# Four of eight gate and up quads as seven block products, and half of the other quads' low parts made by an adding DMA

## The chip, the cores and the metric

The kernel runs on one core of a Trainium2 chip. The metric is the device time of one execution in microseconds (us), as the median of several runs; a profile is taken of one more execution.

## What is computed

A trunk of two layers over 256 tokens with a model width of 2048, in float32. Layer 0 has a gated mixer and a pooling mixer, layer 1 latent attention; the change touches neither. Each layer ends in a SwiGLU, and that is where the change is made:

```python
D_MODEL = 2048; SEQ = 256
D_FF = -(-8 * D_MODEL // (3 * 256)) * 256      # 5632

def swiglu(h, w_gate, w_up, w_down):
    return (jax.nn.silu(h @ w_gate) * (h @ w_up)) @ w_down

for layer in range(DEPTH):                     # DEPTH = 2
    ...
    x = x + mix
    x = x + swiglu(rmsnorm(x, g_ffn[layer]), w_gate[layer], w_up[layer], w_down[layer])
return rmsnorm(x, g_final)
```

## The kernel before, in words

**Split operands.** TensorE multiplies in the type `F32R`. To keep float32 accuracy every operand is a pair: a high part `wh`, the value rounded to `F32R`, and a low part `wl`, the value minus its high part. ScalarE (ACT) writes the high part and VectorE (DVE) the low part (`split_raw`, lines 95 to 104, in pieces of up to 1024 columns). A product of two pairs is three matmuls: high by high, high by low, low by high (`token_product`, lines 205 to 209; every one of them 128 by 128 by 512 columns here).

**Quads.** Gate and up are computed in *columns*: a column is 512 of the 5632 outputs of gate and the same 512 of up, for all 256 tokens. There are 11 columns in each layer, cut into parts of 4, 4 and 3 (`PARTS`); after each part the rows of `w_down` that belong to it are multiplied (`into_trunk`). The 2048 inputs of a column are taken in eight *quads* j = 0 to 7 of 256 inputs. A quad is a 2 by 2 matrix of input blocks (x11, x21, x12, x22, 128 tokens by 128 inputs each) times a 2 by 2 matrix of weight blocks (b11, b12, b21, b22, 128 inputs by 512 outputs each). Done directly it takes eight block products, 24 matmuls. The quads in `SEVEN` (3, 5, 7) are done by Winograd's form with seven block products, 21 matmuls: `quad_seven` (lines 471 to 485) makes the sums t1, t3, t2, t4 of weight blocks on DVE and splits them too, and `put_pair` (lines 253 to 270) makes the sums s1 to s4 of input blocks once per layer, in the tile `forms` (it has the name `ckv` in the profile). Four accumulators c11, c12, c21, c22 hold the column (tiles `mm`) and four more, p1, p6, p5, p7 (tiles `sm`), the shared products; eight additions on DVE (`L520`) put them together at the column's end, with copies out of PSUM on ACT before them (`L519`).

**What sets the order.** One generator, `chunks_of`, walks over all quads of gate and up and all chunks of `w_down` in the order of use. For each it issues one load of 1024 KB into `raw` (three buffers) from the SP queue and splits it, and it runs two chunks ahead of the matmuls. High and low parts have six buffers each. A buffer is handed out in the order in which buffers come free, so each piece takes the place of the sixth piece before it, as soon as the matmuls that read that one are through.

```python
    whs = pool("whs", 6)
    wls = pool("wls", 6)
    ...
            while len(ready) <= AHEAD and todo:
                src, split = todo.pop(0)
                raw = raws.tile([P, 2 * SPLIT], F32, name="raw")
                nc.sync.dma_start(out=raw, in_=src)
                ready.append(split(raw))
```

After a column its hidden block is turned by transposes on TensorE into two `sm` tiles of PSUM and split from there into `hid` (`L581`, `L582`). These wait in a list, `pending`, and are emitted in the next column: after quads 1 and 2 two each, if so many are there (line 554). The order on each engine is set by a scheduler when the program is built; it is fixed in the program.

Of the kernel before, what the change touches and what calls it, by code (L numbers as in the profile page):

```python
# [21 lines left out]

SEVEN = (3, 5, 7)
AHEAD = 2
# [8 lines left out]
def trunk(ctx: ExitStack, tc: tile.TileContext, a: dict, out: bass.AP):  # L33
# [210 lines left out]
    def into_trunk(w, k0, nk, moving, g, sums, chunks=None, scaled=None):  # L244


        def turn(m, src):

            def put(pt):
                for j in range(2):  # L250
                    split_into(xs[:, m + j, :], pt[:, j * T:(j + 1) * T], gain(g, m + j))

            def put_pair(pt):
                xg = ev([2, T])
                for j in range(2):
                    nc.scalar.activation(out=xg[:, j, :], in_=pt[:, j * T:(j + 1) * T], func=AF.Copy, scale=gain(g, m + j))
                nc.scalar.activation(out=xs[:, m:m + 2, :T], in_=xg, func=AF.Copy)
                nc.vector.tensor_tensor(out=xs[:, m:m + 2, T:], in0=xg, in1=xs[:, m:m + 2, :T].bitcast(F32), op=ALU.subtract)
                if m // 2 not in SEVEN:
                    return  # L260
                a11, a21, a12, a22 = xg[:, 0, :P], xg[:, 0, P:], xg[:, 1, :P], xg[:, 1, P:]
                f = ev([4, P])
                s1, s2, s3, s4 = (f[:, i, :] for i in range(4))
                nc.vector.tensor_tensor(out=s1, in0=a21, in1=a22, op=ALU.add)
                nc.vector.tensor_tensor(out=s2, in0=s1, in1=a11, op=ALU.subtract)
                nc.vector.tensor_tensor(out=s3, in0=a11, in1=a21, op=ALU.subtract)
                nc.vector.tensor_tensor(out=s4, in0=a12, in1=s2, op=ALU.subtract)
                q = scaled["forms"][:, SEVEN.index(m // 2), :, :, :]
                nc.scalar.activation(out=q[:, 0, :, :], in_=f, func=AF.Copy)
                nc.vector.tensor_tensor(out=q[:, 1, :, :], in0=f, in1=q[:, 0, :, :].bitcast(F32), op=ALU.subtract)  # L270

            turned(src, put_pair if scaled else put)
# [52 lines left out]
    def forms():  # L325

        return big.tile([P, len(SEVEN), 2, 4, P], F32R, name="ckv")

# [141 lines left out]

    def quad_seven(raw):

# [13 lines left out]

    def quad_eight(raw):
        parts = split_raw(raw, 2048)
        return dict(zip(("b11", "b12", "b22", "b21"), (block(parts, i) for i in range(4))))

    def chunks_of(layer):
# [4 lines left out]
        for n in PARTS:  # L496
# [3 lines left out]
            for c in range(4):  # L500
                for i in range(0, 4 * n, 4):
                    todo.append((wd[c, :, (4 * at + i) * 512:(4 * at + i + 4) * 512], lambda raw: split_raw(raw, 2048)))
            at += n
        ready = []
        for n in range(len(todo)):
            while len(ready) <= AHEAD and todo:
                src, split = todo.pop(0)
                raw = raws.tile([P, 2 * SPLIT], F32, name="raw")
                nc.sync.dma_start(out=raw, in_=src)
                ready.append(split(raw))  # L510
            yield ready.pop(0)

    def feed_forward(layer, sums, scaled, g_next):
# [7 lines left out]
        for part, n in enumerate(PARTS):  # L521
            hid = hidden()
            for c in range(n):
# [8 lines left out]
                for j in range(KD // 2):  # L532
# [4 lines left out]
                    if j not in SEVEN:  # L537
                        for xk, bg, bu in (((x11, x21), "b11", "b12"), ((x12, x22), "b21", "b22")):
                            for x_t, pg, pu in ((xk[0], c11, c12), (xk[1], c21, c22)):
                                sum_into(pg, x_t, w[bg], False)  # L540
                                sum_into(pu, x_t, w[bu], pu is c22 and xk[0] is x12 and j == max(set(range(KD // 2)) - set(SEVEN)))
                    else:
                        if j == SEVEN[0]:
                            p1, p6, p5, p7 = (ps_sm.tile([P, 512], F32, name="sm") for _ in range(4))
                        q = forms[:, SEVEN.index(j)]
                        s1, s2, s3, s4 = ((q[:, 0, i, :], q[:, 1, i, :]) for i in range(4))
                        sum_into(c11, x12, w["b21"], lasting)
# [4 lines left out]
                        sum_into(p5, s1, w["t1"], lasting)  # L552
                        sum_into(p7, s3, w["t3"], lasting)
                    if j in (1, 2):
                        next_pending(2)
                    if j == KD // 2 - 2:
                        e22 = copy(c22)
# [266 lines left out]
```

## Time and profile before

| | |
|---|---|
| median of 3 runs | 1942.32 us (1941.19 to 1942.67) |
| profiled execution, its own time | 1942.75 us |
| its span in the profile | 1940.9 us, so 1.85 us lie around the span |
| TensorE (PE) busy | 1921.9 us, 99% of the span, 9110 matmuls |
| DVE, ACT, POOL busy | 75%, 55%, 1% |
| loads on the SP queue | 53.5% of the 16 DMA engines' span |

The duration of a matmul in the profile covers its whole way through the array, so several overlap; what one costs is the distance between two starts. The same holds for DVE and ACT: an instruction starts a little before the one ahead of it is down as ended. A row of a timeline gives the start, the duration, the engine, the line, the operation, tiles out and in, and in square brackets the idle time before it and what ended it. "High" and "low" rows of weights are `L101` and `L102`.

### The profile page before, as it was taken

What the parts mean: (1) busy time and instruction counts of PE and PEld (TensorE: products, weight loads), DVE (VectorE), ACT (ScalarE), POOL (GpSimd) and SP (SyncE); (2) the same over time, 40 slices, a digit from 0 to 9 for tenths busy, and PEclk for the clock granted to TensorE, in tenths of its full rate; (3) what the DMA queues carried; (4) which work ended last, traced back from release to release, by engine and by line L of the source; (5) the groups of instructions that cost most, each with busy time, mean ns of one, the idle gap of its engine ahead of it and who ended that gap; (6) DMA issues with size and microseconds to landing.
All of it is one profiled execution on the core that took longest, in us unless ns stands there. A gap on an engine that the chain in (4) does not pass through costs nothing.

```text
span 1940.9 us, 23494 instructions
## 1 busy us (share of the span) xinstructions
PE 1921.9 (99%) x9110; PEld 1610.7 (83%) x9110; DVE 1448.9 (75%) x1793; ACT 1066.0 (55%) x1424; POOL 10.1 (1%) x26
## 2 busy tenths in 40 slices
PE   9999999999999999999999999999999999999997
PEld 7888888888888888888889988888888888888886
DVE  6685589985688965887676755899856889658884
ACT  6554666563456643555554755665634566435562
POOL 0000000000000000000000000000000000000000
PEclk9999999999999999999999999999999999999998
DMA  8565545565555555456455235455655556655562
GB/s 310 174 215 197 195 160 209 195 213 194 179 195 195 210 201 190 179 195 217 175 194 175 96 135 184 171 208 188 214 194 183 187 199 211 210 181 177 208 242 87
DMA packets 54688, 370.94 MB, mean 191 GB/s; under 512 B 6320, under 2 KB 7856, under 8 KB 10544
## 3 DMA queue, kind: packets, MB, share of 16 engines
q1 hardware_dynamic: 52560, 364.93, 53.5%
q10 hardware_dynamic: 2016, 4.51, 0.6%
q8 instruction: 71, 1.16, 0.2%
q14 instruction: 41, 0.34, 0.0%
HBM read 367.32 MB, written 2.10 MB: 190 GB/s over the span
## 4 chain that ended last, share of the span: by engine, by line
PE 97%; DVE 1%; DMA 1%; ACT 1%; issue 0%; POOL 0%; ACTq 0%; SPq 0%; POOLq 0%
PE mm L207 24%; PE mm L209 24%; PE mm L208 24%; PE mm L131 5%; PE sm L209 3%; PE sm L208 3%; PE sm L207 3%; PE mm L132 2%; PE sm L241 2%; PE mm L363 1%; PE mm L364 1%; PE mm L137 1%; PE mm L362 1%; PE mm L136 1%; PE mm L138 1%; DMA raw<-in_w_v 1%
## 5 line engine op out<-in xcount | busy, mean ns | idle before, releaser
L102 DVE TENSOR_TENSOR wl<-raw,wh 128x1024 fp32r<-128x1024 f32 (+1 forms) x692 | 802.7, 1165 | 342.6 <-ACT wh L101 338.9
L101 ACT ACTIVATE wh<-raw 128x1024 fp32r<-128x1024 f32 (+1 forms) x692 | 695.1, 1013 | 538.4 <-PE mm L209 458.8
L207 PE MATMUL mm<-wh,xs 128*128 128x512 f32 x1012 | 395.2, 391 | 0.0
L209 PE MATMUL mm<-wh,xs 128*128 128x512 f32 x1012 | 393.9, 389 | 0.0
L208 PE MATMUL mm<-wl,xs 128*128 128x512 f32 x1012 | 393.8, 389 | 0.0
L207 PE MATMUL mm<-wh,hid 128*128 128x512 f32 x960 | 375.5, 391 | 0.0
L209 PE MATMUL mm<-wh,hid 128*128 128x512 f32 x960 | 373.6, 390 | 0.0
L208 PE MATMUL mm<-wl,hid 128*128 128x512 f32 x960 | 373.6, 389 | 0.0
L209 PEld LDWEIGHTS mm<-wh,xs 128*128 128x128 f32 x1012 | 189.9, 188 | 39.5
L207 PEld LDWEIGHTS mm<-wh,xs 128*128 128x128 f32 x1012 | 190.0, 188 | 39.0
L208 PEld LDWEIGHTS mm<-wl,xs 128*128 128x128 f32 x1012 | 190.0, 188 | 38.8
L209 PEld LDWEIGHTS mm<-wh,hid 128*128 128x128 f32 x960 | 180.2, 188 | 37.5
L207 PEld LDWEIGHTS mm<-wh,hid 128*128 128x128 f32 x960 | 180.2, 188 | 37.0 <-ACT hid L581 0.3
L208 PEld LDWEIGHTS mm<-wl,hid 128*128 128x128 f32 x960 | 180.3, 188 | 36.7
L102 DVE TENSOR_TENSOR wl<-sums,wh 128x1024 fp32r<-128x1024 f32 x132 | 161.3, 1222 | 63.6 <-ACT wh L101 63.6
L101 ACT ACTIVATE wh<-sums 128x1024 fp32r<-128x1024 f32 x132 | 139.4, 1056 | 126.1 <-DVE sums L475 96.6
L131 PE MATMUL mm<-xs,wh 128*128 128x512 f32 x375 | 133.8, 399 | 0.0
L132 PE MATMUL mm<-xs,wl 128*128 128x256 f32 x375 | 104.8, 280 | 0.0
L131 PEld LDWEIGHTS mm<-xs,wh 128*128 128x128 f32 x375 | 70.4, 188 | 15.9 <-DVE xs L170 0.3
L475 DVE TENSOR_TENSOR sums<-raw 128x1024 f32<-128x1024 f32 x66 | 80.5, 1220 | 1.0 <-DMA raw<-in_w_gu 0.5
L520 DVE TENSOR_TENSOR ev<-sm,ev 128x512 f32<-128x512 f32 x110 | 75.6, 688 | 2.6
L207 PE MATMUL sm<-wh,ckv 128*128 128x512 f32 x198 | 77.0, 389 | 0.0
(198 smaller groups left out, 1920.2 us busy)
## 6 DMA issues: line engine op xcount, KB each, us to landing
raw<-in_w_gu SPq DMA_DIRECT2D x176, 1024.0 KB, 4.8
raw<-in_w_d SPq DMA_DIRECT2D x88, 1024.0 KB, 4.8
raw<-in_w_o SPq DMA_DIRECT2D x32, 1024.0 KB, 4.8
raw<-in_w_v SPq DMA_DIRECT2D x11, 1024.0 KB, 6.6
raw<-in_w_z SPq DMA_DIRECT2D x8, 1024.0 KB, 5.0
raw<-in_w_u SPq DMA_DIRECT2D x8, 1024.0 KB, 4.8
raw<-in_w_q SPq DMA_DIRECT2D x6, 1024.0 KB, 4.9
raw<-in_w_ckv SPq DMA_DIRECT2D x4, 1024.0 KB, 4.8
```

Source lines behind the costliest of these rows:

```text
L101: nc.scalar.activation(out=wh[:, :m], in_=raw[:, o:o + m], func=AF.Copy)
L102: nc.vector.tensor_tensor(out=wl[:, :m], in0=raw[:, o:o + m], in1=wh[:, :m].bitcast(F32), op=ALU.subtract)
L131: nc.tensor.matmul(ps, lhsT=wh, rhs=mv, start=first, stop=False)
L132: nc.tensor.matmul(ps[:, :T], lhsT=wl, rhs=mv[:, :T], start=False, stop=last)
L136: nc.tensor.matmul(ps[:, :T], lhsT=wh, rhs=mv[:, :T], start=first, stop=False)
L137: nc.tensor.matmul(ps[:, :T], lhsT=wh, rhs=mv[:, T:], start=False, stop=False)
L207: nc.tensor.matmul(ps, lhsT=hi, rhs=wh, start=first, stop=False)
L208: nc.tensor.matmul(ps, lhsT=hi, rhs=wl, start=False, stop=False)
L209: nc.tensor.matmul(ps, lhsT=lo, rhs=wh, start=False, stop=last)
L241: nc.tensor.transpose(pt[:, o:o + P], src(t, j), ident)
L475: sub = lambda out, p, q: nc.vector.tensor_tensor(out=out, in0=p, in1=q, op=ALU.subtract)
L520: add = lambda out, p, q: nc.vector.tensor_tensor(out=out, in0=p, in1=q, op=ALU.add)
```

## The change

Four things are changed.

1. `SEVEN` becomes (2, 4, 6, 7), so that four quads of a column take seven block products, and 0, 1, 3, 5 (`EIGHT`) take eight.
2. `quad_eight` splits only its first 1024 columns (b11, b12) as before. For the second 1024 (b22, b21) ACT writes the negated high part into `wl`, and a DMA from the POOL queue adds the weights to it, read a second time from DRAM (512 KB each). ACT also writes the high part as before; DVE does nothing for this half. The second half's `wl` is asked for first, ahead of the first half's.
3. In the quads of `SEVEN` the input block x21 is replaced in place by a11 - a21, which is the form s3; `forms` then keeps three forms for each of four quads instead of four for each of three.
4. All of `pending` is emitted after quad 1 (`SEVEN[0] - 1`), and c22 is copied out after quad 5 (`EIGHT[-1]`) instead of quad 6.

```diff
-SEVEN = (3, 5, 7)
+SEVEN = (2, 4, 6, 7)
+EIGHT = tuple(j for j in range(KD // 2) if j not in SEVEN)
...
+                seven = m // 2 in SEVEN
+                if seven:
+                    a11, a21, a12, a22 = xg[:, 0, :P], xg[:, 0, P:], xg[:, 1, :P], xg[:, 1, P:]
+                    f = ev([3, P])
...
+                    nc.vector.tensor_tensor(out=a21, in0=a11, in1=a21, op=ALU.subtract)
...
-        return big.tile([P, len(SEVEN), 2, 4, P], F32R, name="ckv")
+        return big.tile([P, len(SEVEN), 2, 3, P], F32R, name="ckv")
...
-    def quad_eight(raw):
-        parts = split_raw(raw, 2048)
+    def quad_eight(raw, src):
+
+        wh = whs.tile([P, SPLIT], F32R, name="wh")
+        wl = wls.tile([P, SPLIT], F32R, name="wl")
+        nc.scalar.activation(out=wl, in_=raw[:, SPLIT:], func=AF.Copy, scale=-1.0)
+        nc.gpsimd.dma_start(out=wl, in_=src[:, SPLIT:], accum_op=ALU.add)
+        nc.scalar.activation(out=wh, in_=raw[:, SPLIT:], func=AF.Copy)
+        parts = split_raw(raw, SPLIT) + [(wh, wl, SPLIT)]
         return dict(zip(("b11", "b12", "b22", "b21"), (block(parts, i) for i in range(4))))
...
-                        s1, s2, s3, s4 = ((q[:, 0, i, :], q[:, 1, i, :]) for i in range(4))
+                        s1, s2, s4 = ((q[:, 0, i, :], q[:, 1, i, :]) for i in range(3))
...
-                        sum_into(p7, s3, w["t3"], lasting)
-                    if j in (1, 2):
-                        next_pending(2)
-                    if j == KD // 2 - 2:
+                        sum_into(p7, x21, w["t3"], lasting)
+                    if j == SEVEN[0] - 1:
+                        next_pending(len(pending))
+                    if j == EIGHT[-1]:
                         e22 = copy(c22)
```

**ACT where one column passes into the next.** The rows of ACT before, from the last pieces of quad 7 of layer 0's second column to the first copy out of PSUM of that column's sums (`raw_2812` is quad 7; `raw_2855` and `raw_2891` are quads 0 and 1 of the third column):

```order
L101 ACTIVATE wh_2830<-sums_2814 128x1024
L101 ACTIVATE wh_2857<-raw_2855 128x1024
L101 ACTIVATE wh_2861<-raw_2855 128x1024
L519 ACTIVATE ev_2889<-mm_2602 128x512
L101 ACTIVATE wh_2893<-raw_2891 128x1024
```

The same place of the changed kernel (`raw_2845` is quad 7; `raw_2893` and `raw_2925` are quads 0 and 1 of the third column; `L497` writes the high part of the second half, `L495` its negated copy into `wl`, `L102` the high part of the first half):

```order
L102 ACTIVATE wh_2859<-raw_2845 128x512
L102 ACTIVATE wh_2863<-sums_2847 128x1024
L497 ACTIVATE wh_2895<-raw_2893 128x1024
L495 ACTIVATE wl_2896<-raw_2893 128x1024
L102 ACTIVATE wh_2900<-raw_2893 128x1024
L497 ACTIVATE wh_2927<-raw_2925 128x1024
L495 ACTIVATE wl_2928<-raw_2925 128x1024
L102 ACTIVATE wh_2932<-raw_2925 128x1024
L529 ACTIVATE ev_2957<-mm_2621 128x512
```

A quad of eight products had two instructions on ACT and has three now, and the negated copy stands behind the high part of the same half; the copy of c22 (`L519`, `ev_2889`) has moved up to quad 7's pieces.

**POOL around the second column of layer 0.** Before, POOL has only small powers here:

```order
L315 TENSOR_TENSOR rtok_1973<-rstd_s_1970,mhalf_102 128x2
L319 TENSOR_TENSOR rback_1975<-rstd_s_1970,half_104 128x2
L315 TENSOR_TENSOR rtok_2573<-rstd_s_2570,mhalf_102 128x2
```

In the changed kernel (the DMAs in order are those of quads 0, 1, 3, 5 of the first column and 0, 1, 3 of the second):

```order
L319 TENSOR_TENSOR rtok_1973<-rstd_s_1970,mhalf_102 128x2
L323 TENSOR_TENSOR rback_1975<-rstd_s_1970,half_104 128x2
L496 DMA wl_2216<-in_w_gu0 128x1024
L496 DMA wl_2227<-in_w_gu0 128x1024
L319 TENSOR_TENSOR rtok_2595<-rstd_s_2592,mhalf_102 128x2
L496 DMA wl_2284<-in_w_gu0 128x1024
L496 DMA wl_2404<-in_w_gu0 128x1024
L496 DMA wl_2530<-in_w_gu0 128x1024
L496 DMA wl_2562<-in_w_gu0 128x1024
L496 DMA wl_2674<-in_w_gu0 128x1024
```

The adding DMAs stand in a row on POOL, four to a column and 88 in all; the one power that stands between them waits for sums that are complete before the first column begins.

**DVE at the start of the second column of layer 0.** In the changed kernel (`raw_2625` is quad 2, now a quad of seven; `wl_2535` and `wl_2567` are the first halves of quads 0 and 1, `L530` the additions of the column that has ended):

```order
L103 TENSOR_TENSOR wl_2535<-raw_2527,wh_2534 128x1024
L479 TENSOR_TENSOR sums_2627<-raw_2625 128x1024
L103 TENSOR_TENSOR wl_2567<-raw_2559,wh_2566 128x1024
L530 TENSOR_TENSOR ev_2598<-sm_2376,ev_2598 128x512
L484 TENSOR_TENSOR sums_2627<-sums_2627,raw_2625 128x512
L530 TENSOR_TENSOR ev_2604<-sm_2376,ev_2604 128x512
L103 TENSOR_TENSOR wl_2630<-raw_2625,wh_2629 128x1024
```

The sums of quad 2, which need its load, now stand ahead of the low part of quad 1 and of all additions; before, quad 2 had no sums, and those of quad 3 stood behind the additions.

## Rows read from the trace of the kernel before

**Rows 1.** The page: busy time of each engine, and the chain that ended last.
```profile
PE 1921.9 (99%) x9110; PEld 1610.7 (83%) x9110; DVE 1448.9 (75%) x1793; ACT 1066.0 (55%) x1424; POOL 10.1 (1%) x26
...
PE 97%; DVE 1%; DMA 1%; ACT 1%; issue 0%; POOL 0%; ACTq 0%; SPq 0%; POOLq 0%
```
**Rows 2.** What PE waited for: total us, times, longest (longest total first).
```profile
PE mm L362 <- ACT wh L101: 2.9, 2, 2.3
PE sm L86 <- DVE ones L73: 1.0, 1, 1.0
```
**Rows 3.** Timeline of PE in a column: quads 0, 1, transposes, quad 2.
```profile
333.34 0.39 PE L207 MATMUL mm<-wh,xs 128*128 128x512 f32 x1
...
343.99 0.39 PE L209 MATMUL mm<-wh,xs 128*128 128x512 f32 x1
344.23 1.03 PE L241 MATMUL sm<-ident,qn 128*128 128x128 f32 x8
345.02 0.48 PE L207 MATMUL mm<-wh,xs 128*128 128x512 f32 x1
```
**Rows 4.** Busy us of each engine in that column; clock, DMA share, GB/s last.
```profile
core 0: us, PE busy (x) PEld busy (x) DVE busy (x) ACT busy (x) POOL busy (x), PEclk, DMA share, GB/s
...
333.40:375.80 42.40, 42.40 (x193) 35.20 (x192) 38.66 (x44) 25.36 (x32) 0.00 (x0) 1.00 0.55 197
```
**Rows 5.** Timeline of DVE: additions of a column's end, then one quad of seven.
```profile
336.95 0.69 DVE L520 TENSOR_TENSOR ev<-sm,ev 128x512 f32<-128x512 f32 x1
337.56 1.28 DVE L520 TENSOR_TENSOR ev<-ev 128x512 f32<-128x512 f32 x2
...
351.30 1.22 DVE L475 TENSOR_TENSOR sums<-raw 128x1024 f32<-128x1024 f32 x1
352.44 2.35 DVE L102 TENSOR_TENSOR wl<-raw,wh 128x1024 fp32r<-128x1024 f32 x2
354.71 0.68 DVE L480 TENSOR_TENSOR sums<-sums,raw 128x512 f32<-128x512 f32 x1
355.43 0.69 DVE L475 TENSOR_TENSOR sums<-raw,sums 128x512 f32<-128x512 f32 x1
357.33 1.23 DVE L102 TENSOR_TENSOR wl<-sums,wh 128x1024 fp32r<-128x1024 f32 x1 [1.21 <-ACT wh L101]
358.47 0.68 DVE L102 TENSOR_TENSOR wl<-raw,wh 128x512 fp32r<-128x512 f32 x1
359.07 1.22 DVE L102 TENSOR_TENSOR wl<-sums,wh 128x1024 fp32r<-128x1024 f32 x1
360.21 1.22 DVE L102 TENSOR_TENSOR wl<-raw,wh 128x1024 fp32r<-128x1024 f32 x1
```
**Rows 6.** Timeline of ACT: the high parts of the same quad.
```profile
356.23 1.06 ACT L101 ACTIVATE wh<-sums 128x1024 fp32r<-128x1024 f32 x1 [3.01 <-DVE sums L475]
357.20 0.62 ACT L101 ACTIVATE wh<-raw 128x512 fp32r<-128x512 f32 x1
357.72 1.05 ACT L101 ACTIVATE wh<-sums 128x1024 fp32r<-128x1024 f32 x1
358.67 1.04 ACT L101 ACTIVATE wh<-raw 128x1024 fp32r<-128x1024 f32 x1
```
**Rows 7.** DMA issues: count, KB each, median us from issue to landing.
```profile
raw<-in_w_gu SPq DMA_DIRECT2D x176, 1024.0 KB, 4.8
...
raw<-in_w_v SPq DMA_DIRECT2D x11, 1024.0 KB, 6.6
...
out<-x SPq DMA_DIRECT2D x2, 512.0 KB, 3.4
```
**Rows 8.** DMA queues in that column: packets, MB, share of 16 engines.
```profile
q1 hardware_dynamic: 1142, 8.31, 55.1%
```
**Rows 9.** Who waited for the loads of line 509: us, times.
```profile
  ACT wh L101: 1.4, 1
  DVE sums L475: 0.5, 2
```

More of the change, by code (lines that the diff above doesn't have):

```diff
@@ L256, in put_pair @@
                     nc.scalar.activation(out=xg[:, j, :], in_=pt[:, j * T:(j + 1) * T], func=AF.Copy, scale=gain(g, m + j))
+                seven = m // 2 in SEVEN
+                if seven:
+                    a11, a21, a12, a22 = xg[:, 0, :P], xg[:, 0, P:], xg[:, 1, :P], xg[:, 1, P:]
+                    f = ev([3, P])
+                    s1, s2, s4 = (f[:, i, :] for i in range(3))
+                    nc.vector.tensor_tensor(out=s1, in0=a21, in1=a22, op=ALU.add)
+                    nc.vector.tensor_tensor(out=s2, in0=s1, in1=a11, op=ALU.subtract)
+                    nc.vector.tensor_tensor(out=a21, in0=a11, in1=a21, op=ALU.subtract)
+                    nc.vector.tensor_tensor(out=s4, in0=a12, in1=s2, op=ALU.subtract)
                 nc.scalar.activation(out=xs[:, m:m + 2, :T], in_=xg, func=AF.Copy)
                 nc.vector.tensor_tensor(out=xs[:, m:m + 2, T:], in0=xg, in1=xs[:, m:m + 2, :T].bitcast(F32), op=ALU.subtract)
-                if m // 2 not in SEVEN:
+                if not seven:
                     return
[L261 to L267, printed above, removed]
                 q = scaled["forms"][:, SEVEN.index(m // 2), :, :, :]
@@ L468, in trunk, with quad_seven @@
     into_trunk(a["w_o0"], 0, KD, ab, "ffn0", sums, scaled=scaled)
-    def quad_seven(raw):
+    def quad_seven(raw, _):
         sums = big.tile([P, 2048], F32, name="sums")
@@ L501, in chunks_of @@
                 for i in range(0, 4 * n, 4):
-                    todo.append((wd[c, :, (4 * at + i) * 512:(4 * at + i + 4) * 512], lambda raw: split_raw(raw, 2048)))
+                    todo.append((wd[c, :, (4 * at + i) * 512:(4 * at + i + 4) * 512], lambda raw, _: split_raw(raw, 2048)))
             at += n
@@ L509, in chunks_of @@
                 nc.sync.dma_start(out=raw, in_=src)
-                ready.append(split(raw))
+                ready.append(split(raw, src))
             yield ready.pop(0)
@@ L540, in feed_forward @@
                                 sum_into(pg, x_t, w[bg], False)
-                                sum_into(pu, x_t, w[bu], pu is c22 and xk[0] is x12 and j == max(set(range(KD // 2)) - set(SEVEN)))
+                                sum_into(pu, x_t, w[bu], pu is c22 and xk[0] is x12 and j == EIGHT[-1])
                     else:
```

## The prediction

> **What bounds the kernel now.** I read the page's busy times and chain first [rows 1]: PE is busy 99% of the span, and the chain that ended last is 97% PE. Then PE's waits [rows 2]: the longest total is 2.9 us, at the start of the program; in the feed-forward PE waits for nothing. So a matmul less is time less, if everything that feeds PE stays ahead. What a matmul costs stands in PE's timeline [rows 3]: from 333.34 to 343.99 lie 48 matmuls of quads 0 and 1, that is 47 steps in 10.65 us, 0.2266 us each. [...] DVE has under 4 us to spare per column; that is why each further quad of seven must be paid for on DVE.
>
> **Matmuls removed.** A quad of seven has 21 matmuls for 24. One more such quad in each of 22 columns removes 66 matmuls: 66 x 0.2266 = 15.0 us [rows 3]. All of it lies on the path that sets the end. A quad of eight takes 24 x 0.2266 = 5.44 us, one of seven 4.76, the transposes 0.79 (344.23 to 345.02), so a column becomes 4 x 5.44 + 4 x 4.76 + 0.79 = 41.6 us.
>
> **DVE.** By starts [rows 5] a 1024-wide instruction takes 1.14 us, a 512-wide one 0.60. Each of four quads of eight keeps one low part instead of two, and the fifth is gone: 10 become 4, -6.8 us. The further quad of seven adds four 1024-wide and three 512-wide ones, +6.4. DVE falls from 38.66 to about 38.2 us in a column that is 0.8 us shorter: as full as before, no term.
>
> **ACT.** A high part takes 0.96 us by starts, 0.52 for 512 [rows 6]. The quads of eight go from 10 to 12 instructions (+1.9), the further quad of seven adds 3 x 0.96 + 0.52 = 3.4. ACT goes from 25.4 to 30.7 of 41.6 us: room is left, no term. The forms (point 3) have one 128-wide difference and its split fewer per quad, in four quads instead of three, once per layer beside PE: nothing. Should that cover go, it is under 2 us a layer.
>
> **DMA load.** Eight loads take 55.1% of 42.4 us [rows 8], 23.4 us, 2.9 each. Of 41.6 us 18.2 remain for four accumulations: they fit if one keeps the engines busy for under 4.5 us. A 512 KB transfer at the loads' rate takes 1.46 us; the accumulation reads two such streams.
>
> **The new wait.** The low part of a second half is now a chain: PE frees a buffer, ACT writes high part and negated copy (2 x 0.96 and some 0.2 of hand-over; from DVE's end at 356.12 to ACT's start at 356.23 are 0.11 [rows 5, 6]), POOL issues, the DMA lands, and PE needs it at the quad's 14th matmul. Behind the wait on POOL stand only further accumulations; behind it on PE stands everything. I call L the time from POOL's issue to landing. With buffers handed out six back, the slack for L follows by counting matmuls:
>
> - Quad 0 takes the buffer that quad 6 of the column before frees with its 15th matmul: 6 + 21 + 13 = 40 matmuls, 9.07 us, less 2.1 for ACT and 0.3 for the copy ahead of it there: 6.7 us. This holds in the 16 columns that follow another column directly.
> - Quad 1: freed by matmul 6 of quad 7; 52 matmuls, but ACT comes to it 0.5 us late: 9.2 us.
> - Quad 3: freed by matmul 12 of quad 1; 46 matmuls and the transposes, 11.2 less 2.1: 9.1 us. In 6 columns (second, sixth and tenth of each layer) ACT's order has the first half's high part ahead of the negated copy, and that waits for quad 1's end: 6.4 us.
> - Quad 5: matmul 12 of quad 3, 46 matmuls: 8.3 us.
> - First columns of a part have w_down or w_o chunks before them, of 24 matmuls each: quads 0 and 1 have over 14 us.
>
> How long is L? No row of before shows an accumulation or a DMA from POOL. From below, a 512 KB transfer alone: 3.4 us; three such passes one after the other (read, read, write): 10.2. Nearest is a transfer with as many bytes read, 1024 KB: 4.8 us, and where such loads were crowded by others, 6.6 [rows 7]. Since loads run beside the accumulations here (one is issued within 2 us of quad 0's), I take 6.6. That is under 6.7, and over 6.4 by 0.2 in 6 columns: 1.2 us. I add 2 us for columns at the edge.
> [...]
>
> **Sum.** The profiled execution took 1942.75 us, 0.4 above the median of the three. 1942.75 - 15.0 + 1.2 + 2 = **1931 us**.
>
> **Rival 1, accumulations that land late: slower.** Each column stalls by L - 6.7 at quad 0 and, in 6, by L - 6.4 at quad 3. Over both layers the stall is 16 (L - 6.7) + 6 (L - 6.4); it eats the whole 15.0 us at L = 7.2 to 7.3. At L = 8 it is 20.8 + 9.6 = 30, time 1958; at 9 quad 5 (10 columns over 8.3, and two first columns) adds 8: 61 in all, 1989; at 10.2 quads 3 and 5 take part everywhere, about 102, time 2030. For it: the threshold is only 0.6 above my L, a second queue is served beside the loads, and quads 0 and 1 issue their accumulations 2.9 us apart. Against it: 45% of the DMA engines' time is free [rows 8].
>
> **Rival 2, POOL cannot issue while DVE works: slower.** DVE is busy 38 of 41.6 us, and its instructions last up to 1.22 us [rows 5]. If the writing of descriptors has to wait for the one running, L grows by up to 1.2 to 7.8: 16 x 1.1 + 6 x 1.4 = 26, time 1954. [...]
>
> **Rival 3, the load of quad 2 comes late on DVE: no change.** Quad 2 is now one of seven, and DVE's order puts its first sum ahead of quad 1's low part and of the eight additions. Its buffer comes free some 6.0 us before the column's start, so it lands at -1.2 with 4.8 us; then quad 1's low part ends at +1.2, and additions (8 x 0.61), two products of gate and up (1.3), the rest of quad 2 (5.2), quad 3's low part (1.1) and two of `hid` (1.3) end at 15.1. p7, whose PSUM bank the transposes used, starts at 10.88 + 0.79 + 18 x 0.2266 = 15.75. So 0.6 us of slack; before, p7 came in quad 3, over 5 us later. If the load takes 6.6 us, DVE is 1.7 late and PE stalls 1.1 in 16 columns, 17 us: 1945. Against it: DVE waited for loads for 0.5 us in all [rows 9].
>
> **Chances.** The forecast (L under 7.0, the load of quad 2 in time) 0.56. Rival 1 has 0.26, rival 2 0.06, rival 3 0.12. A measurement of this kernel can tell about 0.2%, 3.9 us, from no change: faster is then a stall of under 11 us, same one of 11 to 19. Of rival 3 I count 0.07 as same and 0.05 as slower; of rival 1 0.03 as same. So faster 0.56, same 0.10, slower 0.34. The forecast's own range is 1926 to 1938. The low end is the whole 15.0 and nothing else, with the spread of the runs; the high end, 1990, is rival 1 at L = 9, and beyond it I leave some 0.1.
>
> **What would show it.** Right: 9044 matmuls, PE's waits for `wl` of line 496 near zero, accumulations landing in 5 to 7 us, columns of 41.6 us, DVE's waits still on ACT. Wrong by rival 1: PE waits at the 14th matmul of quad 0 (`L209`, low part) for a POOL DMA, the same in each second and later column of a part. By rival 2: time between ACT's negated copy and the DMA's first packet, and the landing itself short. By rival 3: DVE idle before `L479` on a load, and PE waiting at p7 or p5 in quad 2. A longer distance than 0.2266 between matmuls, or loads at 8 us or more, would break the sum itself.

## The result, and the profile after

| kernel | median of the runs, us | least to most | runs | profiled span |
|---|---|---|---|---|
| before | 1942.49 | 1941.19 to 1942.76 | 4 | 1940.9 |
| changed | 2012.3 | 2008.24 to 2014.94 | 4 | 2011.7 |

The ratio is 1.0358, interval 1.0343 to 1.0374: 70 us slower, where the prediction had 1931 and its range ended at 1990. In line numbers of the changed kernel: L208 to L210 are the three matmuls of a product, L209 the one that reads a low part; L102 and L103 write high and low parts, L479 and L484 the sums of a quad of seven, L495 the negated copy, L496 the adding DMA, L497 the high part beside it, L530 the additions at a column's end.

First the page of the changed kernel: busy times, queues, the chain by engine, what stood ahead of the product with a low part, and the adds' median from issue to landing.

```profile
PE 1935.5 (96%) x9044; PEld 1609.2 (80%) x9044; DVE 1448.1 (72%) x1825; ACT 1182.4 (59%) x1558; POOL 86.5 (4%) x114
...
q0 software_dynamic: 12672, 46.14, 13.0%
...
PE 85%; DMA 11%; issue 2%; DVE 1%; ACT 1%; SPq 0%; POOL 0%; ACTq 0%; POOLq 0%
...
L209 PE MATMUL mm<-wl,xs 128*128 128x512 f32 x880 | 354.5, 403 | 55.8 <-DMA wl<-in_w_gu 55.8
...
L496 POOL DMA_DIRECT2D wl<-in_w_gu x88 | 76.3, 867 | 1258.4 <-ACT wl L495 875.4
L479 DVE TENSOR_TENSOR sums<-raw 128x1024 f32<-128x1024 f32 x88 | 107.6, 1223 | 28.0 <-DMA raw<-in_w_gu 26.4
...
wl<-in_w_gu POOLq DMA_DIRECT2D x88, 512.0 KB, 6.8
```

Against [rows 1]: the 66 matmuls are gone (9110 to 9044) and DVE's total is what it was, as predicted. But the chain, 97% PE before, has 11% DMA, PE waits 55.8 us for the adding DMAs where it waited for nothing in the feed-forward [rows 2], and DVE's first sums wait 26.4 us for loads that cost it 0.5 before [rows 9]. The 88 adds kept 16 engines busy for 13.0% of 2011.7 us, that is 2.97 us each: about the two streams of 1.46 that the prediction assumed. Their median landing was 6.8 us, near the 6.6 that it took.

One wait shows most of it. PE's timeline of the changed kernel at the start of the third column:

```profile
337.50 0.39 PE L210 MATMUL mm<-wh,xs 128*128 128x512 f32 x1
337.73 0.39 PE L208 MATMUL mm<-wh,xs 128*128 128x512 f32 x1
340.61 0.69 PE L209 MATMUL mm<-wl,xs 128*128 128x512 f32 x1 [2.50 <-DMA wl<-in_w_gu]
341.10 0.63 PE L210 MATMUL mm<-wh,xs 128*128 128x512 f32 x1
341.53 1.06 PE L208 MATMUL mm<-wh,xs 128*128 128x512 f32 x2
```

The matmul that waits is the *fifth* of quad 0 (the quad starts at 337.05), not the 14th. The scheduler put the second half's first product second on PE in ten columns (third, fourth, seventh, eighth and last of each layer). And after the wait matmuls start 0.43 us apart. The windows around it, PE's count in the first brackets, the granted clock before the DMA share:

```profile
333.94:337.35 3.41, 3.41 (x17) 2.83 (x16) 1.34 (x2) 3.41 (x5) 0.86 (x1) 1.00 1.00 318
337.35:340.74 3.39, 0.90 (x5) 0.43 (x4) 2.88 (x3) 3.39 (x6) 0.86 (x1) 1.00 0.97 221
340.74:344.15 3.41, 3.41 (x9) 2.64 (x10) 3.41 (x6) 0.96 (x2) 0.00 (x0) 0.50 1.00 309
344.15:347.56 3.41, 3.41 (x16) 2.80 (x15) 3.41 (x7) 0.75 (x2) 0.00 (x0) 1.00 1.03 341
```

PE was busy 0.90 of 3.39 us, and then the granted clock is 0.50 for 3.41 us with 9 matmuls for 16. The feed-forward has twelve such stretches, two of them of 6.83 us, 47.8 us in all, where before had none there; by the distances 0.2266 and 0.427 they lose up to 47.8 x 0.47 = 22 us. Each begins within a wait of PE (four) or at most 1.5 us after the end of one (eight), but only twelve of the 24 waits counted below have one: one of 2.1 us has, one of 2.7 us has not.

Why the add was late: ACT's timeline ahead of it, and POOL's.

```profile
330.00 1.06 ACT L102 ACTIVATE wh<-sums 128x1024 fp32r<-128x1024 f32 x1 [1.67 <-DVE sums L479]
...
332.44 1.05 ACT L497 ACTIVATE wh<-raw 128x1024 fp32r<-128x1024 f32 x1
333.39 1.04 ACT L495 ACTIVATE wl<-raw 128x1024 fp32r<-128x1024 f32 x1
```

```profile
334.72 0.86 POOL L496 DMA_DIRECT2D wl<-in_w_gu  x1 [18.07 <-ACT wl L495]
337.56 0.86 POOL L496 DMA_DIRECT2D wl<-in_w_gu  x1 [1.98 <-ACT wl L495]
```

ACT came to the copy late because it sat behind quad 7's sums, which it got late from DVE. The add itself took 5.5 us from its issue to its last packet (5.85 to the landing that DMA rows count), less than the 6.6 reckoned; issued 3.2 us before its matmul was due, it could not be in time. No wait of PE in the feed-forward is for DVE here: DVE's lateness reaches PE through ACT's late copy.

All waits counted by the starts of the matmuls (over 0.4 us): 24, 59.5 us, all for adding DMAs. Ten are quad 0 as above (2.5 to 4.6). Six are quad 1 and six quad 3 of the second, sixth and tenth column (1.5 to 2.8 and 2.5 to 2.7), two others 1.5 together. Quad 1's adds have their last packet 10.6 to 11.5 us after the issue there, quad 3's 8.3 to 8.5, with their first packet 4.3 to 4.8 us after it; of the 24 adds whose first packet comes at 1.6 to 1.8, 23 have the last at 5.0 to 6.2 (the landing of the DMA rows is some 0.3 us later). So 59.5 + 22, and 4 in smaller gaps, make the 85.8 us that separate the two spans once the 15.0 of the matmuls are counted (70.8 + 15.0).

### The profile page after: what moved, and what is told of

Its sections match the earlier page's. It is cut to its first block, busy times and chain, and to the rows that moved or that the text cites. A ratio compares the mean times of both kernels' runs of the same rounds, so it can differ in the third digit from the quotient of the medians.

```text
span 2011.7 us, 23853 instructions
## 1 busy us (share of the span) xinstructions
PE 1935.5 (96%) x9044; PEld 1609.2 (80%) x9044; DVE 1448.1 (72%) x1825; ACT 1182.4 (59%) x1558; POOL 86.5 (4%) x114
## 4 chain that ended last, share of the span: by engine, by line
PE 85%; DMA 11%; issue 2%; DVE 1%; ACT 1%; SPq 0%; POOL 0%; ACTq 0%; POOLq 0%
PE mm L209 21%; PE mm L210 21%; PE mm L208 20%; DMA wl<-in_w_gu 10%; PE mm L132 4%; PE sm L209 3%; PE sm L208 3%; PE sm L210 3%; PE mm L133 2%; PE sm L242 1%; DMA raw<-in_w_v 1%; PE mm L138 1%; PE mm L139 1%; PE mm L137 1%; PE mm L367 1%
## 5 line engine op out<-in xcount | busy, mean ns | idle before, releaser
L103 DVE TENSOR_TENSOR wl<-raw,wh 128x1024 fp32r<-128x1024 f32 (+1 forms) x604 | 684.3, 1137 | 360.7 <-ACT wh L102 357.0
L102 ACT ACTIVATE wh<-raw 128x1024 fp32r<-128x1024 f32 (+1 forms) x604 | 595.0, 989 | 459.0 <-PE mm L210 376.1
L209 PE MATMUL mm<-wl,xs 128*128 128x512 f32 x880 | 354.5, 403 | 55.8 <-DMA wl<-in_w_gu 55.8
L208 PE MATMUL mm<-wh,hid 128*128 128x512 f32 x960 | 374.5, 391 | 0.1
L209 PE MATMUL mm<-wl,hid 128*128 128x512 f32 x960 | 374.5, 390 | 0.0
L210 PE MATMUL mm<-wh,hid 128*128 128x512 f32 x960 | 374.4, 391 | 0.0
L210 PE MATMUL mm<-wh,xs 128*128 128x512 f32 x880 | 350.3, 398 | 0.0
L208 PE MATMUL mm<-wh,xs 128*128 128x512 f32 x880 | 347.3, 402 | 0.0
L102 ACT ACTIVATE wh<-sums 128x1024 fp32r<-128x1024 f32 x176 | 185.8, 1056 | 159.6 <-DVE sums L479 126.9
L103 DVE TENSOR_TENSOR wl<-sums,wh 128x1024 fp32r<-128x1024 f32 x176 | 215.0, 1222 | 80.3 <-ACT wh L102 63.4
L209 PEld LDWEIGHTS mm<-wl,xs 128*128 128x128 f32 x880 | 169.9, 193 | 100.9 <-DMA wl<-in_w_gu 66.9
L208 PEld LDWEIGHTS mm<-wh,hid 128*128 128x128 f32 x960 | 180.4, 188 | 37.4 <-ACT hid L591 0.8
L210 PEld LDWEIGHTS mm<-wh,hid 128*128 128x128 f32 x960 | 180.3, 188 | 37.3
L209 PEld LDWEIGHTS mm<-wl,hid 128*128 128x128 f32 x960 | 180.4, 188 | 36.6
L208 PEld LDWEIGHTS mm<-wh,xs 128*128 128x128 f32 x880 | 170.7, 194 | 38.6 <-ACT ev L529 1.9
L210 PEld LDWEIGHTS mm<-wh,xs 128*128 128x128 f32 x880 | 170.1, 193 | 35.4
L496 POOL DMA_DIRECT2D wl<-in_w_gu x88 | 76.3, 867 | 1258.4 <-ACT wl L495 875.4
L479 DVE TENSOR_TENSOR sums<-raw 128x1024 f32<-128x1024 f32 x88 | 107.6, 1223 | 28.0 <-DMA raw<-in_w_gu 26.4
L495 ACT ACTIVATE wl<-raw 128x1024 fp32r<-128x1024 f32 x88 | 92.2, 1048 | 25.5 <-PE mm L209 25.5
L497 ACT ACTIVATE wh<-raw 128x1024 fp32r<-128x1024 f32 x88 | 91.9, 1045 | 3.8 <-PE mm L210 2.0
```

The source lines that it names most:

```text
L102: nc.scalar.activation(out=wh[:, :m], in_=raw[:, o:o + m], func=AF.Copy)
L103: nc.vector.tensor_tensor(out=wl[:, :m], in0=raw[:, o:o + m], in1=wh[:, :m].bitcast(F32), op=ALU.subtract)
L208: nc.tensor.matmul(ps, lhsT=hi, rhs=wh, start=first, stop=False)
L209: nc.tensor.matmul(ps, lhsT=hi, rhs=wl, start=False, stop=False)
L210: nc.tensor.matmul(ps, lhsT=lo, rhs=wh, start=False, stop=last)
L479: sub = lambda out, p, q: nc.vector.tensor_tensor(out=out, in0=p, in1=q, op=ALU.subtract)
```

## The experiments

The theories after the result. **A**: the adds are late, and late alone. **B**: the seven-quads' place and DVE's order cost something without any add. **C**: the adds' traffic costs without any wait for them. All times below are medians; before was 1942.57 to 1942.93 beside them.

### The parts apart

**a1_no_add**, the change without its DMA:

```diff
-        nc.gpsimd.dma_start(out=wl, in_=src[:, SPLIT:], accum_op=ALU.add)
```

> The changed kernel without the 88 adding DMAs; what is left out is the addition of the weights, so the low part of the second half is the negated high part alone. Theory A (the loss is PE waiting for adds that land late, 24 waits of 59.5 us in all, and the half clock after them, 44 us at half speed or 22 us): nothing is left to wait for, 66 matmuls fewer show whole, 1926 to 1931 us. Theory B (the loss is in the new order: four quads of seven crowd DVE and ACT, and the adds only show it): PE then waits for DVE or ACT instead, 1945 us or more.

Measured 1961.1, ratio 1.0094 (1.0079 to 1.0109). With no add at all it is 33.5 us over the 1942.6 - 15.0 = 1927.6 that 66 matmuls should give. B is right for a large part, and the other 51 come with the adds.

**a2_not_read**, the adds kept, but PE reads something else:

```diff
-        parts = split_raw(raw, SPLIT) + [(wh, wl, SPLIT)]
+        parts = split_raw(raw, SPLIT) + [(wh, wh, SPLIT)]
```

> The changed kernel with all 88 adding DMAs, but TensorE multiplies with the high part of the second half in place of its low part, so PE never waits for an add; what is left out is the product with the low part of half of the weights of quads 0, 1, 3 and 5. Theory A: the DMA traffic by itself costs nothing, 1927 to 1934 us. Rival C (the adds take DMA time from the loads, which then land late): loads of w_gu still at 5.2 us median or more, DVE waits for them, 1940 us or more.

Measured 1987.1, 26 us over a1. That spoke for C, but the run isn't clean: an unread `wl` goes out again at once, and its next writers wait for the DMA, ACT 22.0 us and DVE 20.7. No weight is put on it.

**a3_pe_order**, eight-quads' products held in program order on PE:

```diff
...
-        nc.tensor.matmul(ps, lhsT=hi, rhs=wh, start=first, stop=False)
+        m = nc.tensor.matmul(ps, lhsT=hi, rhs=wh, start=first, stop=False)
+        if kept_order:
+            tc.keep_in_program_order(m)
...
```

> The changed kernel with the products of quads 0, 1, 3 and 5 held in program order on PE, so that the second half of quad 0 is first read at its 14th matmul in all columns, not at the 5th in ten of them. Theory A: the ten waits of 2.6 to 4.6 us at quad 0 shrink by up to 9 x 0.227 = 2.0 us each, and most of their half clock goes; but quad 1 of those columns gets earlier by as much and may wait up to 1 us: 1975 to 1995 us. If the order on PE does not matter (the add is late in any case and only waits elsewhere): 2005 to 2015.

Measured 2009.8, ratio 1.0342 (1.0327 to 1.0358): no clear difference from the change, though quad 0's second half is again its last. The waits moved: 42.4 us for adds in 29 pieces instead of 55.8 in 25. PE's order alone was not the fault. PE's row for the adds (L211 is the product with a low part here):

```profile
PE mm L211 <- DMA wl<-in_w_gu: 42.4, 29, 3.3
```

**a4_seven_alone**, four seven-quads with every low part made by DVE (`quad_eight` as it was):

> Part 1 of the change alone: four quads of seven products, every low part made by DVE, no adding DMA. DVE then has about 38.2 + 4 x 1.14 = 42.8 us of work in a column of 41.6. Theory A says nothing of adds here: PE waits for DVE, columns of 42.8 to 44 us, 1940 to 1965 us; if DVE's work is hidden all the same: 1927 to 1932.

Measured 2000.9, 36 us above the upper expectation, and PE waits 28.4 us for high parts, which ACT cannot write before DVE's sums are there:

```profile
PE mm L208 <- ACT wh L102: 28.4, 16, 2.0
```

After waits 17.0 us stand at the half clock, some 8 us lost (mean granted clock 0.993, before's 0.996). DVE is far more of a bound than its sum of 42.8 us per column says.

### Place or volume

**c1_low_by_act** writes negated high parts as low parts of both halves of the eight-quads; **c2_odd_sevens** keeps a1's work and moves the seven-quads (c2's edit):

```diff
-SEVEN = (2, 4, 6, 7)
+SEVEN = (1, 3, 5, 7)
...
-        nc.gpsimd.dma_start(out=wl, in_=src[:, SPLIT:], accum_op=ALU.add)
```

> Leaves out the low parts of the weights of quads 0, 1, 3 and 5: ScalarE writes their negated high parts there, both halves, and no DMA adds anything. VectorE loses another four subtractions of 1024 columns per column of gate and up (38.2 to 33.6 us), ScalarE goes up by four instructions to 34.5 us; the order of the quads and their place stay. Theory D (VectorE's own time per column, its work and some 5 to 6 us in which it waits for ScalarE's rounding and for loads, sets the 44.5 us of most columns of the run without adds): VectorE now needs about 39.8 us, less than TensorE's 41.7, so 1926 to 1934. Rival O (what holds TensorE is where the quads of seven stand, quad 2 soon after the sums at the column's start): no change from 1961, at the least over 1945.

> The run without adds again (leaves out half of the low parts of the four quads of eight), but with quads 1, 3, 5 and 7 as seven block products in place of 2, 4, 6 and 7. The work of each engine is the same. Theory D: the same 1955 to 1966. Rival O: the evenly spread quads of seven give VectorE time between them, 1926 to 1945; quad 1 as a quad of seven could also make it worse, over 1966, since its differences come sooner after the column's end.

Measured 1937.8 and 1933.6 (c2's ratio 0.9953, 0.9938 to 0.9968). Rival O holds for c2: the same work on every engine, 27.5 us less. By point 4 of the change `pending` moves with the place, to after quad 0, and the copy of c22 to after quad 6. c1 came out between its two ends: less DVE work also heals it, for 23 of the 27.5. Both are one thing, DVE's *lead*: how long a low part is ready before PE wants it. DVE's timeline of a1, from quad 7's low parts to quad 2 of the next column (on PE quad 7 starts at 371.12, quad 0 at 376.08, quad 2 at 388.91):

```profile
373.44 1.22 DVE L103 TENSOR_TENSOR wl<-sums,wh 128x1024 fp32r<-128x1024 f32 x1
376.00 1.23 DVE L103 TENSOR_TENSOR wl<-raw,wh 128x1024 fp32r<-128x1024 f32 x1 [1.35 <-ACT wh L102]
378.39 1.23 DVE L479 TENSOR_TENSOR sums<-raw 128x1024 f32<-128x1024 f32 x1 [1.17 <-DMA raw<-in_w_gu]
379.54 1.22 DVE L103 TENSOR_TENSOR wl<-raw,wh 128x1024 fp32r<-128x1024 f32 x1
380.67 1.28 DVE L529 TENSOR_TENSOR ev<-sm,ev 128x512 f32<-128x512 f32 x2
...
387.27 0.68 DVE L479 TENSOR_TENSOR sums<-raw,sums 128x512 f32<-128x512 f32 x1
...
389.32 1.22 DVE L103 TENSOR_TENSOR wl<-sums,wh 128x1024 fp32r<-128x1024 f32 x1
```

And of c2, from quad 7's low parts to the same additions (quad 7 on PE from 369.48 to 374.24):

```profile
367.15 1.22 DVE L103 TENSOR_TENSOR wl<-sums,wh 128x1024 fp32r<-128x1024 f32 x1
368.41 1.23 DVE L479 TENSOR_TENSOR sums<-raw 128x1024 f32<-128x1024 f32 x1
...
370.39 0.69 DVE L479 TENSOR_TENSOR sums<-raw,sums 128x512 f32<-128x512 f32 x1
371.00 2.43 DVE L103 TENSOR_TENSOR wl<-raw,wh 128x1024 fp32r<-128x1024 f32 x2
373.35 0.68 DVE L529 TENSOR_TENSOR ev<-sm,ev 128x512 f32<-128x512 f32 x1
```

In a1 quad 7's last low part is ready at 374.66, when PE is already 3.5 us into the quad: quads 6 and 7, both of seven, have used the lead up. Quad 0's first low part stands behind it on DVE, waits there for ACT's high part, and is ready at 377.23; PE waits for it at its second matmul:

```profile
376.08 0.45 PE L208 MATMUL mm<-wh,xs 128*128 128x512 f32 x1
377.28 0.50 PE L209 MATMUL mm<-wl,xs 128*128 128x512 f32 x1 [0.76 <-DVE wl L103]
```

The 48 matmuls of quads 0 and 1 should take 10.9 us from 376.08, and quad 2 starts 1.9 us late. Its own first sum has waited for its load and started at 378.39, the column's additions have run in between, its last sum ends at 387.95, and PE loses another 0.8 us there. In all columns of a1 PE loses 31 us more than before (by the starts of its matmuls, against 0.2266): 16 in quad 0, 11 in quads 1 and 2, 3 in quads 5 and 7. In c2 quad 7's low parts are ready at 368.37, 1.1 us before the quad starts, and the *next* column's first seven-quad has all its sums by 371.08, before the additions begin.

**f4_ends_together** checks this with quads 1, 3, 6, 7 (no adds):

> No adds (leaves out half of the low parts of the four quads of eight), quads 1, 3, 6 and 7 as seven block products. It tells apart the two things in which 2, 4, 6, 7 (1961.1) and 1, 3, 5, 7 (1933.6) differ. If two quads of seven one behind the other at the column's end use up VectorE's lead before the sums at the column's end: 1950 to 1965. If it is that the first quad of seven, before which the column before is summed and turned, comes as quad 2: 1930 to 1940.

Measured 1954.1. Two seven-quads in a row at the column's end cost 20.5 of the 27.5 us; PE waits for `qn`, the products after those additions:

```profile
PE sm L242 <- DVE qn L584: 13.7, 15, 1.1
```

That is the additions' side of the same lead; in a1 over half was lost at quad 0's own parts. The copy of c22 goes back to after quad 5 with them, and no run parts the two; c1, which has it there too, came within 4.2 us of c2, with less work on DVE.

### The adds in the better place

**e1_odd_add** is the whole change with quads 1, 3, 5, 7; **e4_odd_copy** has a plain copy for the add; **e3_odd_half_loads** cuts the loads in two; **f3_quarter_bytes** adds 256 columns instead of 1024 (first e3's edit, then f3's):

```diff
-                nc.sync.dma_start(out=raw, in_=src)
+                for o in (0, SPLIT):
+                    nc.sync.dma_start(out=raw[:, o:o + SPLIT], in_=src[:, o:o + SPLIT])
...
-        nc.gpsimd.dma_start(out=wl, in_=src[:, SPLIT:], accum_op=ALU.add)
+        nc.gpsimd.dma_start(out=wl[:, :SPLIT // 4], in_=src[:, SPLIT:SPLIT + SPLIT // 4], accum_op=ALU.add)
```

> The change whole, nothing left out, with quads 1, 3, 5 and 7 as the seven block products in place of 2, 4, 6 and 7. Without the adds that place alone gave 1933.6 against 1961.1. Every add's product is now the 14th matmul of its quad in TensorE's order, and the buffer it goes to comes free 47 or more matmuls earlier (10.7 us); less 1 to 2 us for ScalarE's negated copy, an add has 8.5 to 9.5 us from its issue. Theory S (an add costs only what it lands too late): adds that land in 5.1 to 6.0 us, or in 8.3 to 8.5 behind one load, cost nothing, those that land in 10.5 to 11.5 behind two loads 1 to 2.5 us each; with at most six of these and the slow clock behind some, 1934 to 1955. Rival T (the adds' traffic holds the loads back wherever they stand): the adds' 51 us of the change come back to a large part, 1965 to 1985.

> Quads 1, 3, 5, 7 with a plain copy of the weights in place of the adding DMA (leaves out the negated high part, so the low part is the whole weight): the same issue, bytes and places, but one stream of 512 KB instead of a reading of both operands. Theory T2 (the price is the adds' engine time, 2.97 us each against some 1.5 for a copy): landings 1.5 us or more shorter than in the run with adds and half of its excess over 1933.6. Rival Q2 (it is the waiting behind loads): nearly the same landings behind loads (first packet 4 us and more after the issue) and a time within 5 us of the run with adds.

> The run before the last (quads 1, 3, 5, 7, with the adds) with each 1 MB load of gate, up and down as two DMAs of 512 KB, nothing left out. Theory Q (a late add waits behind whole loads in the 16 DMA engines): the add's first packets come sooner, the landings of 8.3 to 11.5 us become at most some 8, and its time is at or below that of the run with whole loads by as much as the late adds cost there, 1932 to 1940. Rival: the order in the engines has nothing to do with the size of a load: the same landings and time as with whole loads; or the double count of loads costs SyncE and the queue time: over that run by 3 or more.

> Quads 1, 3, 5, 7 with adds in all four quads of eight, each over 256 of its 1024 columns (leaves out the weights in the other 768, whose low part stays the negated high part): the same instructions, waits and order on every engine, a quarter of the bytes. Theory B (the adds cost by their bytes, which hold the loads back): the 37 us over the run without adds fall to 10 or less, 1934 to 1944. Rival (the issue, the waits and ScalarE's earlier copy cost it): 1955 to 1970.

Measured 1970.3, 1955.4, 1995.7 and 1933.2; c2 without adds was 1933.6. The place is worth 42 us to the change. Of the 36.7 that the adds still cost, hardly any is a wait for them. PE's waits of e1, and DVE's:

```profile
PE sm L242 <- DVE qn L585: 20.1, 10, 3.6
PE mm L209 <- DMA wl<-in_w_gu: 3.0, 5, 1.1
```

```profile
DVE sums L479 <- DMA raw<-in_w_gu: 46.4, 34, 2.8
```

PE waits for DVE, and DVE for the *loads* (in c2 for 2.7 us). In e1's profiled execution, 1977.9 us and the longest of its four, 23.8 us stand at the half clock after waits, some 11 us lost (mean granted clock 0.991); c2 and f3 have none of it there (0.997 in both). The DMA issues of 600 to 690 us, in e1, in f3 and in c2 (count, KB, median us to landing):

```profile
raw<-in_w_gu SPq DMA_DIRECT2D x11, 1024.0 KB, 7.1
wl<-in_w_gu POOLq DMA_DIRECT2D x7, 512.0 KB, 8.1
```

```profile
raw<-in_w_gu SPq DMA_DIRECT2D x10, 1024.0 KB, 4.9
wl<-in_w_gu POOLq DMA_DIRECT2D x6, 128.0 KB, 3.7
```

```profile
raw<-in_w_gu SPq DMA_DIRECT2D x10, 1024.0 KB, 4.7
```

In this stretch a load takes 7.1 us beside whole adds and 4.7 to 4.9 beside none or a quarter; over the whole run 43 of e1's 176 loads take more than 6 us, in f3 4 and in c2 5 (medians 5.0, 4.8 and 4.8). f3 has the same instructions and dependences as e1 and costs nothing: it is the bytes (theory B of f3), while the share of DMA time in a column pair, from 334 to 419 us, was 0.75 in e1, 0.65 in f3 and 0.56 in c2. A mean share far under 1 hid that loads and adds come in the same few microseconds: of the 25 slices of 3.4 us from 334 to 419, ten are at 0.97 or more in e1, none in f3 (at most 0.94) or c2 (0.91). The copy halves the engine time (7.2% of 1953.2 us, 1.60 us each, against 2.97) and costs 22 of the 37. Halving the loads was wrong: the adds landed no sooner (median 7.1 over the run, 6.0 with whole loads), PE waited 19.4 us for them instead of 3.0, and DVE's first sums waited 77.7 us for loads instead of 46.4. The late first packets of the change came 4.3 to 4.8 us after the issue, with loads on 0.92 or more of the engines' time in the microsecond before; beside no loads the first packet came after 1.56 to 1.61 us, but eight came as soon with loads on 0.73 or more. That a late add waits behind whole loads, and that smaller loads would bring it sooner, was an estimate (theory Q of e3): e3 refutes the second, and no run shows the first.

### Other ways to pay for the low parts

**e2_odd_seven_alone**: quads 1, 3, 5, 7, all by DVE.

> Quads 1, 3, 5 and 7 as seven block products, all low parts by VectorE, no adds, nothing left out: the plain way to four quads. VectorE's work is 42.8 us per column (38.2 and four subtractions of 1.14), over TensorE's 41.7. Theory: VectorE bounds the columns that have no reserve from the stage before: 2 us late each in some 13 of 22 columns at the least, with its waits for ScalarE 4 to 5: 1955 to 1990, below the 2000.9 of the same with 2, 4, 6 and 7. Rival (the place alone is the cause and VectorE's work is no bound): 1928 to 1940.

Measured 1966.0, 35 us under a4 with the place alone. The first two columns of each part are in time, the third and fourth late, as the table at the end of this section shows: DVE's lead comes from the stage before and lasts two columns.

**d1_pool_half** and **d2_pool_all** let GpSimd subtract, in d1 what the DMA added, in d2 both halves:

```diff
-        nc.scalar.activation(out=wl, in_=raw[:, SPLIT:], func=AF.Copy, scale=-1.0)
-        nc.gpsimd.dma_start(out=wl, in_=src[:, SPLIT:], accum_op=ALU.add)
...
+            by = nc.gpsimd if o in (SPLIT,) else nc.vector
+            by.tensor_tensor(out=wl, in0=half, in1=wh.bitcast(F32), op=ALU.subtract)
...
```

(d1's; in d2 it is `o in (0, SPLIT)`.)

> The low part that the DMA made is made by GpSimd instead, by the subtraction that VectorE did before (raw weights less their high part, 128x1024): no negated copy on ScalarE, no adding DMA, nothing left out. VectorE's work is as in the change and in the run without adds. If the adds' late landing and their traffic cost what stands between 1961 and 2012, this gives 1958 to 1968 as long as the subtraction takes GpSimd under about 4 us and does not slow VectorE; if GpSimd and VectorE get in each other's way on SBUF, over 1975. The duration of the GpSimd subtraction is not known from any trace here.

> As the last, but both halves' low parts of quads 0, 1, 3 and 5 are GpSimd's: eight subtractions of 1024 columns per column, nothing left out. VectorE goes to 33.6 us per column as in the run whose low parts ScalarE makes. Theory D: 1926 to 1936 if one subtraction takes GpSimd under about 4 us (eight fit in 41.7 us at 5.2) and neither engine slows the other; if they share a way to SBUF, the subtractions on both get longer by what they overlap, and 1945 to 1990. Rival O: 1950 to 1965.

Measured 2052.1 and 2138.8, the worst of all, with 51 and 146 us at the half clock (mean granted clock 0.984 and 0.962). Groups of d1, of POOL and of DVE (busy, mean ns):

```profile
L500 POOL TENSOR_TENSOR wl<-raw,wh 128x1024 fp32r<-128x1024 f32 x88 | 260.6, 2968 | 1114.9 <-ACT wh L498 1114.9
```

```profile
L479 DVE TENSOR_TENSOR sums<-raw 128x1024 f32<-128x1024 f32 x88 | 185.1, 2104 | 12.5 <-DMA raw<-in_w_gu 12.0
...
L533 DVE TENSOR_TENSOR ev<-sm,ev 128x512 f32<-128x512 f32 x110 | 74.2, 679 | 0.2
```

A subtraction takes GpSimd 2.97 us. DVE's sums take 2.10 in the mean instead of 1.22: 2.71 for the 52 that run beside a subtraction, 1.22 for the 34 that do not. DVE's additions with one operand in PSUM keep their 0.68, the 16 beside a subtraction too. Issuing DMAs from POOL did not do it: L479 took 1223 ns in the changed kernel.

**f2_two_adds** (quads 1, 3, 5, 7, whole adds in quads 0 and 4 alone) and **g1_half_adds** (all four, 512 columns each, DVE the other 512):

> Quads 1, 3, 5, 7 with adds in quads 0 and 4 alone, the low parts of quads 2 and 6 all VectorE's; nothing left out. VectorE's work 40.5 us per column, the adds' bytes halved. Theory M (adds cost by the loads they hold back, VectorE's work by its excess, and both are paid from one lead): between the run with four adds (1970.3) and that with none (1966.0) or below both, 1945 to 1965. Rival: the two add up, half of 37 for the adds and half of 38 for VectorE's work, 1970 to 1975.

> Quads 1, 3, 5, 7 as seven block products in every column, and in the four quads of eight an add over 512 of the second half's 1024 columns, the other 512 by VectorE; nothing left out. VectorE's work is 40.5 us per column, as the mean of the version with two columns of four (40.7), which TensorE never had to wait for; the adds move half the bytes of the change's. If half the bytes are free as a quarter were: 1928 to 1935. If they hold the loads back as the whole did (37 us) in proportion: 1945 to 1965.

Measured 1965.9 and 1951.9. f2 came out just above its first range, no better than e2 without adds: PE waits 13.9 us for its adds and 7.0 for DVE. In g1 DVE's sums wait 11.9 us for loads; since DVE also makes the other half of these low parts there, g1 does not say what half of the bytes cost alone.

**f1_two_columns** spends four seven-quads only where DVE has a lead, in the first two columns of each part, and has no adds:

```diff
+FOUR = 2
+sevens = lambda c: SEVEN if c < FOUR else SEVEN[1:]
```

with SEVEN = (1, 3, 5, 7), quad 1's form kept beside its plain x21. **g2_three_columns** has FOUR = 3 and adds of 256 columns.

> No adds, nothing left out: quads 1, 3, 5 and 7 as seven block products in the first two columns of each part (12 of 22 columns) and 3, 5 and 7 in the others; quad 1 has both its forms and its plain activations, a small copy. In the run with quads 1, 3, 5, 7 in all columns the first two of each part took 41.69 and 41.80 us, or 40.80 and 41.77, against 42.37 and 42.41 or 41.48 before, and the third and fourth were late since VectorE's 42.8 us of work per column had used up its lead from the stage before. Theory (VectorE's work over a part against TensorE's time): 42.8 and 38.7 us by turns make 40.7 per column, and the lead lasts: 12 columns by 0.65 us, 1934 to 1937. Rival: the third column inherits the missing lead: 1938 to 1948.

> Four quads of seven (1, 3, 5, 7) in the first three columns of each part (17 of 22: the last part has three), 3, 5 and 7 in the fourth, and in every quad of eight an add over 256 of its 2048 columns, which was free in the run with a quarter of the bytes; nothing left out. VectorE's work 41.6 us in a column of four, 37.2 in the fourth, 40.5 in the mean of a part of four, but 41.6 in the part of three, whose three columns come one after the other. Theory: 17 columns by 0.65 us, 1931 to 1936; if the third column's lead is gone as in the run with four in all and no adds (2.5 us late there), 1938 to 1950.

f1 measured 1936.2, ratio 0.9966 (0.9954 to 0.9979): it beats both kernels, by 6.5 and 76 us. g2 measured 1946.5: in each part one column of the first three takes 43.2 to 43.8 us for before's 42.37, which is more than the others gain. PE's waits of f1 in the feed-forward are this one row:

```profile
PE sm L244 <- DVE qn L587: 0.7, 1, 0.7
```

The time of the four columns of layer 0's first part, from a column's first matmul to the next one's, in us (worked out from the trace's records):

| column | before | changed | c2, no adds | e1, adds | e2, all by DVE | f1 |
|---|---|---|---|---|---|---|
| first | 42.37 | 41.90 | 41.89 | 41.90 | 41.69 | 41.69 |
| second | 42.37 | 46.84 | 42.04 | 42.42 | 41.80 | 41.81 |
| third | 42.37 | 46.15 | 42.03 | 44.24 | 44.24 | 42.44 |
| fourth | 42.37 | 46.44 | 42.01 | 47.25 | 46.69 | 42.43 |

41.69 is before's 42.37 less 3 x 0.2266: what the prediction reckoned with everywhere.

## Why the prediction was wrong

- **The matmuls** held: 66 fewer, and where nothing waits (e2's and f1's first columns) a column is 0.68 us shorter, 15.0 in all.
- **DVE, "as full as before, no term"**: this is the first step that failed, 33.5 us by a1. In the change itself it shows as the late copy on ACT, so as waits for adds. The sum of DVE's work was right (1448.1 us in all, 1448.9 before). It compared a column's work with a column's time, and a stage so full lives on its lead: which quad's work falls where decides. Place is 27.5 of it (a1 against c2), two seven-quads in a row at the end (with the copy of c22) 20.5 of that. The other 6 are about 0.3 us in each later column of c2; no run takes them apart.
- **Rival 3** had a part of this mechanism, DVE idle before L479 on a load (22.2 us in a1) and quad 2 late, and 0.12. It priced 1945, no change, from the arrival of one load; it did not see that quads 6 and 7 leave DVE with no lead there. In a1 over half of PE's loss falls in quad 0, ahead of the place where the rival looked.
- **The new wait, slack for quad 0 of 6.7 us**: counted to the 14th matmul and from ACT's earliest start. In ten columns it was the fifth matmul, and ACT came about a microsecond later: in the third column 3.2 us were left at the issue, and 5.3 to the 14th matmul, for a landing in 5.85. PE's order could be read beforehand, and was not. a3 shows that with the order mended other waits come up.
- **L = 6.6 us as one number**: the median was 6.8, but landings run from 5.4 us to 11.8 us beside loads. That an add reads two streams agrees with the engine time, 2.97 us against 1.60 for e4's copy, 1.86 times it; every add of the change landed later than the 4.8 us of a 1024 KB load [rows 7]. Rival 1 was the right kind of loss in the change, 59.5 us.
- **DMA load, "they fit if one keeps the engines busy for under 4.5 us"**: 2.97 fits in the mean and still cost 36.7 us in e1, through the loads that came late to DVE. In e1's profiled execution some 11 us of its loss are the clock after these waits. The mean share of the column pair, 0.75 there, did not show the ten slices at 0.97 or more.
- **The clock after a wait** had no term: 22 us in the change, some 1.6 for each 3.41 us at the lower level.
- **Rival 2**, whose wait no row of before showed, is excluded: the 88 issues took 0.86 to 1.05 us, though in 51 of them DVE worked on `raw` beside it for over 0.2 us, and the first packet came 1.56 to 1.61 us after the issue where the DMA engines were free.

In differences of medians, which add up by construction: 1927.6 + 33.5 (DVE) = 1961.1, and 51.2 for the adds, late landings, slow clock and late loads together, make 2012.3. How these 51.2 divide between late adds and late loads in the change's own place stays open; in the better place nearly all come from late loads, with the clock behind the waits they cause.

## What to carry to other kernels

When the engine behind the bound one is 90% full (DVE here: 38.66 of 42.40 us [rows 4]), ask for its lead stage by stage, not for its sum: put heavy steps evenly, away from each other and from the work at a loop's end, and spend more only in the columns that start with a lead. A transfer that fits in the mean DMA share can still delay the loads it runs beside (from 334 to 419 us of e1 the share was 0.75, and a load took 5.5 us for 4.8 in c2); count who shares the same few microseconds. And count slack to the instruction's place in the scheduler's order, which can be read, not to its place in the source.

## What the runs showed of the hardware that was not expected

- Twelve of the change's 24 waits of PE came with a stretch at the granted clock 0.50, ten of 3.41 us and two of 6.83, 47.8 us in all. The length of the wait does not tell which: 2.1 us had one, 2.7 us had none.
- Cutting each 1024 KB load in two made the kernel 25 us slower (e3, 1995.7, against e1, 1970.3), though the bytes were the same.
- A quarter of the adds' bytes was free (f3, 1933.2, against c2, 1933.6), all cost 37 us (e1, 1970.3). With 256 of 1024 columns an add took 3.9 and 3.7 us to land in the medians of the stretches 334 to 419 and 600 to 690 us, against 7.1 and 8.1 for all of them (f3, e1): about half of the time for a quarter of the bytes.
